# Query, key and gate projections as units of seven half-size products

## The chip, the cores and the metric

The kernel runs on one core of a Trainium2 chip. The metric is the device time of one execution, in microseconds. The core's engines are named as the profile names them: PE is TensorE (matrix products), PEld its weight loads, DVE is VectorE, ACT is ScalarE, POOL is GpSimd, SP is SyncE, which here only issues DMAs.

## The reference

One encoder layer for 512 tokens with 2048 features, in fp32:

```python
h = rms_norm(x, norm_mix_w)
q_a, k_a, v_a, q_g, k_g, v_g, r_g, gate_lr = split_cols(h @ w_in, IN_SPLITS)   # 1024,1024,1024,512,512,1024,1024,16
y_a = chunked_band_attention(q_a, k_a, v_a, att_rel_bias)      # 16 heads of 64, chunks of 64, own chunk + 8 before it
o_g = gated_linear_attention(q_g, k_g, v_g, log_a)             # 4 heads, keys of 128, values of 256
y_g = rms_norm(o_g, gla_norm_w) * silu(r_g)                    # the gates meet the GLA outputs here
x = x + concatenate([y_a, y_g]) @ w_out
u_gate, u_val = split(causal_depthwise_conv(rms_norm(x, norm_ffn_w) @ w_ffn_up))   # 2 x 5632 columns
x = x + (gelu(u_gate) * u_val) @ w_ffn_down
g = sigmoid(rms_norm(x, norm_ple_w) @ w_ple_gate)
x = x + g * (p @ w_ple_proj)                                   # per-layer embedding, 256 features
return rms_norm(x, final_norm_w)
```

With 512 tokens and a band of nine chunks of 64 every earlier token is in the band, so each block of 128 queries (`qt` = 0 to 3) meets 128 x (`qt` + 1) keys.

## The kernel before

**Number form.** Every large fp32 product is made of three: each operand is split into a high part (a copy rounded to the type fp32r, by ACT) and a low part (the rest, a subtraction on DVE), and PE forms high x high, high x low and low x high. The activations lie transposed, features on the partitions: 16 tiles of 128 features by 512 tokens.

**First part (0 to about 600 us): full products.** The normalised input is kept as 16 split tiles, `h1`. `vproj` (L218) forms value projections with tokens on the output's partitions, in two column halves `c` of eight weight tiles `kp` each; the products are L240 to L242. `proj` (L127) forms one block of 128 output columns as 16 feature tiles x 3 products of 512 columns, 48 products (`mm3`, L122 to L125). The order is: the GLA values (`Vg`), the low-rank gate, the four GLA heads with two gate blocks (`gate_block`) between, the attention values (`Va`), and then a loop over `b` = 0 to 8. In it block `b` (two heads of 64) gets its query block (`att_q`), the transposes of the probabilities of `b - 1` (`att_transpose`), its key block (`att_k`), the value products of `b - 1` (`att_out`, L496), and its scores and softmax (`att_probs`, L453 to L475), one head after the other; `b` = 8 carries gate blocks 2 and 3 instead of projections. The Tile scheduler orders this part. Each head's queries and keys stand as two stacked halves of 64 partitions: the query tile holds high over low, and for the key's high and low part the same 64 rows twice, both written by ACT or DVE from the projection.

**Border (about 600 to 668 us): a list of blocks in written order.** From here every PE, DVE and ACT instruction is kept in program order (`InOrder`). `blocks` holds, four times, the two weight halves of a gate block and an embedding block `ple` (24 products, `pp`), which it stores to `ppd`. `block_load`, `block_prep` and `block_product` work three, two and no blocks ahead. The lists `before` and `after` hang the rest on the blocks: the multiplication of the GLA outputs by their gates (`gated`), the storing of operands for the next stage (`mix_pair`), and loads and splits of that stage's operands (`wo.load`, `wo.split`).

**Later stages (about 668 us to the end): units of seven half-size products.** A unit takes two blocks of 128 output columns and all 512 tokens as a 2 x 2 block problem and forms it, after Winograd's variant of Strassen's scheme, from seven products instead of eight, each with 256 tokens and half of the features:

```python
PRODUCTS = {"P1": ("L11", "R11", "A"), "P2": ("L12", "R21", "B"), "P6": ("S2", "N2", "A"), "P5": ("S1", "N1", "C"),
            "P7": ("S3", "T3", "A"), "P3": ("S4", "R22", "C"), "P4": ("L22", "T4", "A")}
```

L are weights, S their sums; R are activations, N and T their differences. A product is 8 feature tiles x 3 = 24 matrix products of 256 columns, accumulated in a PSUM bank `accA`, `accB` or `accC`. The seven activation operands are formed once for a stage by `store_pair`, written to DRAM by SP and loaded back (`Stage.load`, `Stage.split`). The weights go through raw pages of 512 KB: `wanted` is the list of loads in order of use, `free` the free pages, and `issue` starts the next load as soon as a page is free. A sum is a plain load from SP and then an adding DMA from POOL's queue onto the same page (L663), or an addition on DVE, as the unit's `sums` says. `prep_high` and `prep_low` split a product's weights two products ahead of it; `collect` adds a finished product to the unit's quarters. The stages are `wo` (w_out), `up`, `dn0` to `dn2` and `pg` (embedding gate). All units' products make up one list `steps`, and `agenda[i]` holds what else is to be issued at step i; its second key says where in the step: 0 before the splits, 1 between the high and the low split, above 1 after the product.

Of the kernel before, what the change touches and what calls it, by code (L numbers as in the profile page):

```python
# [29 lines left out]
            "P7": ("S3", "T3", "A"), "P3": ("S4", "R22", "C"), "P4": ("L22", "T4", "A")}  # L30
# [9 lines left out]
def encoder_block(ctx: ExitStack, tc: tile.TileContext, A, out):  # L40
# [46 lines left out]

    def page(ring, name, dt=F32, shape=(P, 1024)):
        tags = RINGS[ring]
# [127 lines left out]

    def vproj(src, V, start=False):  # L218
        for c in range(2):
            ps = [psum_mm(f"v{c}_{t}") for t in range(TT)]  # L220
            for kp in range(KD // 2):
                first = start and c == 0
                xs = []
                if first and kp > 0:
                    xs.append(load_input(2 * kp))
                hi, lo = wtile(src[c, kp], f"wv{c}_{kp}", 2 if first and kp < 2 else 1,
                               (lambda: xs.append(load_input(0))) if first and kp == 0 else None)
                if first:
                    xs.append(load_input(2 * kp + 1))
                    sq_acc(xs[0], kp == 0)  # L230
                    sq_acc(xs[1], False)
                    if kp == KD // 2 - 1:
                        first_stats()
                for j in range(2):
                    kt = 2 * kp + j
                    wh = hi[:, j * T:(j + 1) * T]
                    wl = lo[:, j * T:(j + 1) * T]
                    for t in range(TT):
                        sl = slice(t * P, (t + 1) * P)
                        nc.tensor.matmul(ps[t], h1[kt][:, 0, sl], wh, start=kt == 0, stop=False)  # L240
                        nc.tensor.matmul(ps[t], h1[kt][:, 0, sl], wl, start=False, stop=False)  # L241
                        nc.tensor.matmul(ps[t], h1[kt][:, 1, sl], wh, start=False, stop=kt == KD - 1)  # L242
            for t in range(TT):
                nc.scalar.activation(V[:, t, c * T:(c + 1) * T], ps[t], AF.Copy, scale=rtok[:, t:t + 1])
# [5 lines left out]
    onorm = []  # L250
# [9 lines left out]
    with ExitStack() as mix:  # L260
        vp = mix.enter_context(tc.tile_pool(name="v", bufs=1, side="right"))

        with ExitStack() as gctx:
            gp = gctx.enter_context(tc.tile_pool(name="gla", bufs=1, side="right"))
            reset = gp.tile([P, T], F32, name="reset")
            nc.gpsimd.memset(reset, 1.0)
            nc.gpsimd.memset(reset.rearrange("p (c j) -> p c j", j=CHUNK)[:, :, 0:1], 0.0)
            causal = gp.tile([P, P], I32, name="causal")
            nc.gpsimd.memset(causal, 1)
            nc.gpsimd.affine_select(causal, causal, pattern=[[1, P]], compare_op=ALU.is_ge, fill=0, base=0, channel_multiplier=-1)  # L270
            attn_t = []
            for i in range(2):
                t = gp.tile([P, T], F32, name=f"attnT{i}")
                nc.gpsimd.memset(t, 0.0)
                attn_t.append(t)

            V = vp.tile([P, TT, 1024], F32, tag="V", name="Vg")
            vproj(A["w_v_g"], V, True)
            up2 = gp.tile([P, T], F32, name="up2")[0:32]
            nc.sync.dma_start(up2, A["gate_up"])  # L280

            gl = page("wr", "wgate_r")
            nc.sync.dma_start(gl[:, :256], A["w_gate"])
            glh = page("wh", "glh", F32R)
            nc.scalar.activation(glh[:, KD * 32:KD * 32 + 96], attn_t[0][:, 0:96], AF.Copy)
            gl3 = gl[:, :256].rearrange("p (k r) -> p k r", r=16)
            g3 = glh[:, :KD * 32].rearrange("p (k r) -> p k r", r=32)
            nc.scalar.activation(g3[:, :, 0:16], gl3, AF.Copy)
            nc.vector.tensor_tensor(g3[:, :, 16:32], gl3, g3[:, :, 0:16].bitcast(F32), ALU.subtract)
            plr = psum_mm("plr")  # L290
            for kt in range(KD):
                w = glh[:, kt * 32:kt * 32 + P]
                nc.tensor.matmul(plr, w, h1[kt][:, 0, :], start=kt == 0, stop=False)
                nc.tensor.matmul(plr, w, h1[kt][:, 1, :], start=False, stop=kt == KD - 1)
            lr = gp.tile([P, T], F32, name="lr")[0:32]
            nc.vector.tensor_tensor(lr, plr[0:32, :], rb[0:32, :], ALU.mult)

            def gt(name, tag, bufs=1, cols=T):
                return gp.tile([P, cols], F32, tag=tag, name=name, bufs=bufs)

            def gla_proj(hd):
                pz = psum_aux("pz")
                nc.tensor.matmul(pz, up2[:, hd * P:(hd + 1) * P], lr, start=True, stop=True)
                b = bgate[:, hd:hd + 1]
                e = gt("e", "e")
                nc.scalar.activation(e, pz, AF.Abs, bias=b)
                nc.scalar.activation(e, e, AF.Exp, scale=-1.0)
                nc.scalar.activation(e, e, AF.Ln, bias=1.0)
                m = gt("lf", "lf")
                nc.vector.tensor_scalar(m, pz, b, 0.0, ALU.add, ALU.min)  # L310
                nc.vector.tensor_tensor(m, m, e, ALU.subtract)
                cs = gt("cs", "cs")
                nc.vector.tensor_tensor_scan(cs, reset, m, 0.0, ALU.mult, ALU.add)
                cs3 = cs.rearrange("p (c j) -> p c j", j=CHUNK)
                last = cs3[:, :, CHUNK - 1:CHUNK]
                eb = gt("eb", "eb", 2)
                nc.scalar.activation(eb, cs, AF.Exp, scale=1.0 / TAU)
                en = gt("en", "en", 2)
                nc.scalar.activation(en, cs, AF.Exp, scale=-1.0 / TAU)
# [830 lines left out]
    for n in range(3):  # L1150
        block_load(n)
# [198 lines left out]
```

## Time and profile before

| | |
|---|---|
| median of 3 runs | 2340.82 us (2331.72 to 2340.89) |
| profiled execution: time, span | 2332.86 us, 2331.2 us |
| mean granted clock of PE | 0.993 |
| busy: PE, PEld | 2294.6 us (98%), 2155.6 us (92%) |
| busy: DVE, ACT, POOL | 1783.8 us (77%), 1231.0 us (53%), 122.7 us (5%) |
| DMA | 473.99 MB, 203 GB/s over the span |

The busy times are of one execution and of engines that work side by side, so they are not added up; the span is the time from the first to the last recorded instruction. "Granted clock" is the share of full speed that the throttle allowed PE. In the rows of groups, `out<-in` are the program's names for the tiles; then come the shapes, the count, the total of busy time, the mean duration in ns, and the idle time before them with what ended it. `L62` is the line of the helper that records all instructions of the part kept in program order. DMA rows give size and median us from issue to landing. In the chain of waits each row is one instruction with its start (us) and the time that it holds in the chain, followed by engine, tile and line; `x48` joins 48 in a row.

### The profile page before, as it was taken

The numbers are of one execution on the slowest core, as the hardware profiler recorded it, in microseconds if no ns is written. First come the engines' busy times: TensorE is split into PE (matmuls) and PEld (weight loads), VectorE is DVE, ScalarE is ACT, GpSimd is POOL, SyncE is SP. The second block draws the span as 40 slices with busy tenths as digits, with TensorE's granted clock in tenths as the row PEclk, the third lists the DMA queues.
The fourth block names the chain that finished last, engine by engine and source line by source line (L and its number), as shares of the span: only waits on it lengthen the run. The fifth ranks groups of instructions, "written<-read, shape, count | busy, mean of one in ns | idle before, by whom it ended". The sixth has DMA issues, their size and how long they took to land.

```text
span 2331.2 us, 42270 instructions
## 1 busy us (share of the span) xinstructions
PE 2294.6 (98%) x16924; PEld 2155.6 (92%) x16924; DVE 1783.8 (77%) x2459; ACT 1231.0 (53%) x1807; POOL 122.7 (5%) x156
## 2 busy tenths in 40 slices
PE   9999999999999999999999999999999999999996
PEld 8878887777789999999999999999999999999995
DVE  6256326656568898999888888888898787998887
ACT  6344225445455565555555555555564554656655
POOL 0000000000000010100000000000000100000000
PEclk9999999999999999999999999999999999999998
DMA  5222222222687987777777777777866967879994
GB/s 204 84 73 73 100 100 97 92 95 78 228 293 255 283 263 205 213 218 221 213 215 209 217 202 221 208 216 198 260 215 226 313 214 243 295 253 329 282 277 153
DMA packets 172821, 473.99 MB, mean 203 GB/s; under 512 B 18736, under 2 KB 58928, under 8 KB 172624
## 3 DMA queue, kind: packets, MB, share of 16 engines
q1 hardware_dynamic: 148112, 392.64, 47.3%
q0 software_dynamic: 20160, 72.36, 17.4%
q10 hardware_dynamic: 4352, 6.29, 0.8%
q8 instruction: 132, 2.16, 0.4%
q14 instruction: 65, 0.53, 0.1%
HBM read 404.11 MB, written 65.01 MB: 201 GB/s over the span
## 4 chain that ended last, share of the span: by engine, by line
PE 92%; DVE 3%; ACT 2%; DMA 1%; issue 1%; SPq 0%; DVEq 0%; ACTq 0%; POOL 0%; POOLq 0%
PE accA L62 37%; PE accC L62 19%; PE accB L62 9%; PE v L240 2%; PE v L241 2%; PE v L242 2%; PE pr L62 2%; PE pqa L123 1%; PE pqa L124 1%; PE pka L125 1%; PE pqa L125 1%; PE pka L123 1%; PE pka L124 1%; PE pp L62 1%; PE py L496 1%
## 5 line engine op out<-in xcount | busy, mean ns | idle before, releaser
L62 DVE TENSOR_TENSOR wl<-s,wh 128x1024 fp32r<-128x1024 f32 (+1 forms) x317 | 379.3, 1197 | 58.0 <-ACT wh L62 57.6
L62 DVE TENSOR_TENSOR wl<-l,wh 128x1024 fp32r<-128x1024 f32 (+1 forms) x268 | 319.5, 1192 | 48.9 <-ACT wh L62 48.4
L62 ACT ACTIVATE wh<-l 128x1024 fp32r<-128x1024 f32 (+1 forms) x268 | 276.9, 1035 | 146.2 <-PE accC L62 99.0
L62 ACT ACTIVATE wh<-s 128x1024 fp32r<-128x1024 f32 (+1 forms) x317 | 327.4, 1033 | 27.4 <-DVE s L62 11.9
L62 ACT ACTIVATE u<-accA 128x256 f32<-128x256 f32 x254 | 96.2, 379 | 352.8 <-PE accA L62 352.7
L62 DVE TENSOR_TENSOR s<-s,l 128x1024 f32<-128x1024 f32 (+1 forms) x168 | 200.5, 1193 | 0.6 <-DMA s<-in_w_dn 0.6
L62 PE MATMUL accA<-up_T,wh 128*128 128x256 f32 x1408 | 178.8, 279 | 0.0
L62 PEld LDWEIGHTS accA<-up_T,wh 128*128 128x128 f32 x1408 | 170.3, 188 | 0.0
L62 DVE SCALAR_TENSOR_TENSOR cv<-u,cw,cv 128x511 f32<-128x511 f32 (+1 forms) x176 | 131.6, 748 | 3.1
L663 POOL DMA_DIRECT2D s<-in_w_up x88 | 75.1, 853 | 791.8 <-DMA s<-in_w_up 371.1
L119 DVE TENSOR_TENSOR wv_l<-wv_r,wv_h 128x1024 fp32r<-128x1024 f32 (+1 forms) x34 | 39.5, 1161 | 84.3 <-ACT wv_h L118 84.2
L240 PE MATMUL v<-wv_h,h 128*128 128x512 f32 x256 | 100.4, 392 | 0.0
L242 PE MATMUL v<-wv_h,h 128*128 128x512 f32 x256 | 100.0, 391 | 0.0
L241 PE MATMUL v<-wv_l,h 128*128 128x512 f32 x256 | 99.6, 389 | 0.0
L62 PE MATMUL accA<-up_T,wl 128*128 128x256 f32 x704 | 96.6, 279 | 0.0
L62 PE MATMUL accB<-up_R,wh 128*128 128x256 f32 x704 | 91.0, 281 | 2.0 <-DVE up_R L62 1.3
L62 PE MATMUL accA<-dn_T,wh 128*128 128x256 f32 x704 | 90.6, 280 | 1.1 <-ACT wh L62 1.1
L62 PE MATMUL accA<-up_R,wh 128*128 128x256 f32 x704 | 89.8, 280 | 0.0
L62 PE MATMUL accC<-up_N,wh 128*128 128x256 f32 x704 | 89.4, 279 | 0.0
L62 PE MATMUL accC<-up_R,wh 128*128 128x256 f32 x704 | 89.4, 279 | 0.0
L62 PE MATMUL accA<-up_N,wh 128*128 128x256 f32 x704 | 89.4, 279 | 0.0
L62 PEld LDWEIGHTS accB<-up_R,wh 128*128 128x128 f32 x704 | 86.3, 189 | 2.6 <-DVE up_R L62 1.5
(394 smaller groups left out, 5280.2 us busy)
## 6 DMA issues: line engine op xcount, KB each, us to landing
l<-in_w_up SPq DMA_DIRECT2D x132, 512.0 KB, 5.2
s<-in_w_up SPq DMA_DIRECT2D x88, 512.0 KB, 4.7
s<-in_w_up POOLq DMA_DIRECT2D x88, 512.0 KB, 5.6
l<-in_w_dn SPq DMA_DIRECT2D x56, 448.0 KB, 5.1
l<-in_w_out SPq DMA_DIRECT2D x28, 512.0 KB, 4.7
l<-in_w_dn SPq DMA_DIRECT2D x28, 512.0 KB, 5.8
l<-in_w_ple_gate SPq DMA_DIRECT2D x24, 512.0 KB, 6.8
g_R<-cv SPq DMA_DIRECT2D x66, 128.0 KB, 4.5
```

What stands on the lines that cost most here:

```text
L62: ins = f(*args, **kw)
L119: nc.vector.tensor_tensor(lo[:, c], raw[:, c], hi[:, c].bitcast(F32), ALU.subtract)
L123: nc.tensor.matmul(po, whi, act[:, 0, :], start=start, stop=False)
L124: nc.tensor.matmul(po, whi, act[:, 1, :], start=False, stop=False)
L125: nc.tensor.matmul(po, wlo, act[:, 0, :], start=False, stop=stop)
L240: nc.tensor.matmul(ps[t], h1[kt][:, 0, sl], wh, start=kt == 0, stop=False)
L241: nc.tensor.matmul(ps[t], h1[kt][:, 0, sl], wl, start=False, stop=False)
L242: nc.tensor.matmul(ps[t], h1[kt][:, 1, sl], wh, start=False, stop=kt == KD - 1)
L496: nc.tensor.matmul(py[s * 64:(s + 1) * 64, kt * P:T], Va[:, kt, c0:c0 + 64], PT[s][:, kt, kt * P:T], start=kt == 0, stop=kt == TT - 1)
L663: nc.gpsimd.dma_start(t, src("L22" if name == "S1" else "L11"), accum_op=ALU.add)
```

## The change

* The 16 query and key blocks become eight units of seven half-size products: unit `u` takes query block `u` and key block `u` as its two blocks of columns. The eight gate blocks become four units. They form a new first stage `in` (`front`), with units one after the other, six raw pages (r0 to r5) and the banks b0 to b2 for the products, b3 for the attention output and b4 to b7 for the rest. The rings of the other pages are cut for its time (`FRONT_RINGS`).
* Its seven activation operands are formed while the second column half of the GLA values runs: `input_pair(k)` scales x in place by the norm's weight and its reciprocal root `rb`, and `store_pair` writes seven operands for each of eight pairs (56 stores of 128 KB).
* During the attention values (`Va`) operand tiles R11, R21 and N2 are loaded back and split (`operand_step`); N1, T3, R22 and T4 are loaded after the last of those products (`operands_left`) and split in the first steps.
* Values and GLA outputs go through DRAM: `Va` is written there and read back for each block (`load_v`), the GLA outputs are written and read back at their gate units (`load`).
* The attention of block `b` is an agenda of its unit (`attend`): high halves by ACT (`high`), low halves by DVE (`low`), the second copy of the key halves by four DMAs on POOL's queue (`double`), and then three groups of query tiles, `TILES`, each for both heads: scores, softmax, scaling, transposes, copy to SBUF, value products.
* Two embedding blocks (step `PP`) stand ahead of the stage's units, and two behind them. The hand-written block list and the loop over `b` go. The rows of w_out are laid out in another order, so that a pair of operands holds blocks 2m and 2m + 1.

The later stages stay as they are. The core of the diff:

```diff
--- before.py
+++ after.py
-RINGS = {"wr": ("r0", "r1", "r2"), "wh": ("h0", "h1", "h2"), "wl": ("l0", "l1", "l2"), "u": ("u2", "u3", "u0", "u1"),
-         "c": ("c1", "c2", "c0"), "x": ("x0", "x1")}
+RINGS = {"wr": ("r0", "r1", "r2"), "wh": ("h0", "h1", "h2"), "wl": ("l0", "l1", "l2")}
+FRONT_RINGS = {"u": ("u0", "u1"), "c": ("c0",), "x": ("r6",)}
+BACK_RINGS = {"u": ("u2", "u3", "u0", "u1"), "c": ("c1", "c2", "c0"), "x": ("x0", "x1")}
...
-    def gate_block(j):
-        pr = psum_mm("pr")
-        proj(pr, [A["w_blk"][24 + j, i] for i in range(2)], h1, f"wr{j}")
-        r = tp.tile([P, T], F32, tag="sq", name="r")
-        nc.vector.tensor_tensor(r, pr, rb, ALU.mult)
-        nc.scalar.activation(r, r, AF.Silu)
-        nc.vector.tensor_tensor(onorm[j], onorm[j], r, ALU.mult)
...
-            def att_q(b):
-                pq = psum_mm("pqa")
-                proj(pq, [A["w_blk"][b, i] for i in range(2)], h1, f"wqa{b}")
-                qf = ap.tile([P, T], F32, tag="qkf", name="qf")
-                nc.vector.scalar_tensor_tensor(qf, pq, 0.125, rb, ALU.mult, ALU.mult)
-                Q = [ap.tile([P, T], F32R, tag=f"Q{s}", name=f"Q{s}") for s in range(2)]
-                for s in range(2):
-                    a, z = s * 64, 64 - s * 64
-                    nc.scalar.activation(Q[s][a:a + 64], qf[a:a + 64], AF.Copy)
-                    nc.vector.tensor_tensor(Q[s][z:z + 64], qf[a:a + 64], Q[s][a:a + 64].bitcast(F32), ALU.subtract)
...
-            def att_k(b):
-                pk = psum_mm("pka")
-                proj(pk, [A["w_blk"][8 + b, i] for i in range(2)], h1, f"wka{b}")
-                kf = ap.tile([P, T], F32, tag="qkf", name="kf")
-                nc.vector.tensor_tensor(kf, pk, rb, ALU.mult)
-                Kh = [ap.tile([P, T], F32R, tag=f"Kh{s}", name=f"Kh{s}") for s in range(2)]
-                Kl = [ap.tile([P, T], F32R, tag=f"Kl{s}", name=f"Kl{s}") for s in range(2)]
-                for s in range(2):
-                    a, z = s * 64, 64 - s * 64
-                    nc.scalar.activation(Kh[s][a:a + 64], kf[a:a + 64], AF.Copy)
-                    nc.scalar.activation(Kh[s][z:z + 64], kf[a:a + 64], AF.Copy)
-                    nc.vector.tensor_tensor(Kl[s][a:a + 64], kf[a:a + 64], Kh[s][a:a + 64].bitcast(F32), ALU.subtract)
-                    nc.vector.tensor_tensor(Kl[s][z:z + 64], kf[a:a + 64], Kh[s][a:a + 64].bitcast(F32), ALU.subtract)
...
-    free = ["r8"] + [f"r{i}" for i in range(3, 8)]
+    free = [f"r{i}" for i in (3, 4, 5)]
-    banks = [f"b{i}" for i in range(6)]
+    banks = [f"b{i}" for i in range(3)]
...
+    def embedding(unit):
+        hi, lo = unit.w["PP"]
+        for i in range(4):
+            if i % 2 == 0:
+                o = (early[0].tile([P, 1024], F32, tag="pp_o", name="pp_o", bufs=4) if unit.u < 2 else page("c", "pp_o"))
+                o = o.rearrange("p (s t) -> p s t", s=2)
+            pp = psum_aux("pp")
+            for k in range(2):
+                w = slice((i * 2 + k) * P, (i * 2 + k + 1) * P)
+                product3(pp, hi[:, w], lo[:, w], ps_[0][:, k], k == 0, k == 1)
+            act.activation(o[:, i % 2, :], pp, AF.Copy)
+            if i % 2:
+                m = 4 * unit.u + i - 1
+                nc.scalar.dma_start(ppd[m % 8:m % 8 + 2, m // 8].rearrange("m p t -> p m t"), o)
...
+    TILES = ((3,), (2,), (1, 0))
...
+        def high():
+            for n in ("Q", "Kh", "Kl"):
+                for s in range(2):
+                    M[n, s] = tile_(f"{n}{s}", T, F32R)
+            for s in range(2):
+                a = slice(s * 64, s * 64 + 64)
+                act.activation(M["Q", s][a], o[a, 0, :], AF.Copy, scale=0.125)
+                act.activation(M["Kh", s][a], o[a, 1, :], AF.Copy)
+        def low():
+            for s in range(2):
+                a, z = slice(s * 64, s * 64 + 64), slice(64 - s * 64, 128 - s * 64)
+                vec.scalar_tensor_tensor(M["Q", s][z], o[a, 0, :], 0.125, M["Q", s][a].bitcast(F32), ALU.mult, ALU.subtract)
+                vec.tensor_tensor(M["Kl", s][a], o[a, 1, :], M["Kh", s][a].bitcast(F32), ALU.subtract)
+        def double():
+            for s in range(2):
+                a, z = slice(s * 64, s * 64 + 64), slice(64 - s * 64, 128 - s * 64)
+                for n in ("Kh", "Kl"):
+                    nc.gpsimd.dma_start(M[n, s][z], M[n, s][a])
+        def scores(h):
+            for s in range(2):
+                psc = M["psc", s, h] = psum_aux("psc")
+                for i, qt in enumerate(TILES[h]):
+                    w = slice(256 * i, 256 * i + max(P * (qt + 1), 256))
+                    nn = w.stop - w.start
+                    ql = M["Q", s][:, qt * P:(qt + 1) * P]
+                    ten.matmul(psc[:, w], ql, M["Kh", s][:, :nn], start=True, stop=False)
+                    ten.matmul(psc[:, w], ql, M["Kl", s][:, :nn], start=False, stop=True)
...
+        def normal(h):
+            for s in range(2):
+                for qt in TILES[h]:
+                    sc, mx = M["sc", s, qt], M["mx", s, qt]
+                    vec.reciprocal(mx[:, 3:4], mx[:, 2:3])
+                    vec.tensor_scalar(sc, sc, mx[:, 3:4], None, ALU.mult)
+        def turn(h):
+            for s in range(2):
+                ptr = M["ptr", s] = psum_aux("ptr")
+                for i, qt in enumerate(TILES[h]):
+                    for kt in range(qt + 1):
+                        ten.transpose(ptr[:, (2 * i + kt) * P:(2 * i + kt + 1) * P], M["sc", s, qt][:, kt * P:(kt + 1) * P], ident)
...
+        def values(h):
+            if h == 0:
+                M["y"] = pp_.tile([P, T], F32, tag="b3", name="py")
+            for i, qt in enumerate(TILES[h]):
+                for kt in range(qt + 1):
+                    for s in range(2):
+                        o = (2 * i + kt) * P
+                        ten.matmul(M["y"][s * 64:(s + 1) * 64, qt * P:(qt + 1) * P], M["V"][:, kt, s * 64:(s + 1) * 64],
+                                   M["PT"][:, s, o:o + P], start=kt == 0, stop=kt == qt)
...
+        items = [(2, 0, load_e), (2, 2, high), (3, 1, low), (3, 3, double), (4, 1, mask), (5, 0, load_v), (11, 1, result)]
+        if b % 2:
+            items.append((12, 1, lambda: store_pair(mixd, b // 2, ypair[0][:, 0, :], ypair[0][:, 1, :])))
+        for h in range(3):
+            items += [(t + h, k, lambda f=f, h=h: f(h)) for t, k, f in (
+                (5, 6, scores), (6, 1, soft), (7, 1, normal), (7, 5, turn), (8, 1, evict), (8, 4, values))]
+        return items
...
+        return [(0, 0, load), (0, 1, lambda: act.activation(unit.o, unit.o, AF.Silu)), (0, 2, times), (0, 3, pair)]
...
+    front = Stage("in", list(range(12)), 8, h1d, front_weights, lambda u: (attend if u.u < 8 else after_gates)(u), "dma",
+                  "dma", single=True)
+    embed = [Stage("pp", us, 8, None, lambda u, q: A["w_ple_proj"][u], lambda u: [], "dma", "dma", single=True)
+             for us in ([0, 1], [2, 3])]
+    for u in embed[0].units + embed[1].units:
+        u.order, u.uses, u.made = ("PP",), dict(L11=1), set()
...
+    stages[:0] = [embed[0], front, embed[1]]
...
+    for n, op in enumerate(("T3", "R22", "T4")):
+        for g in range(2):
+            agenda[n + g * (n == 2)].append((3, lambda op=op, g=g: front.split(op, g)))
...
+            def input_pair(k):
+                for i in (k, k + 8):
+                    x = xslot(i, "")
+                    vec.scalar_tensor_tensor(x, x, nmix[:, i:i + 1], rb, ALU.mult, ALU.mult)
+                store_pair(h1d, k, xslot(k, ""), xslot(k + 8, ""), gp.tile([P, 1024], F32, tag="tp", name="tp", bufs=2))
+            for c in range(2):
+                vproj(A["w_v_g"], c, lambda t: V[:, t, c * T:(c + 1) * T], c == 0, input_pair if c else None)
...
+    def operand_step(kp):
+        if kp > 1:
+            front.split(*X0[kp - 2])
+        if kp == 3:
+            embedding_split(raws["p"], early[0].tile([P, 2, 1024], F32R, tag="ps", name="ps"))
+            issue()
+    def operands_left():
+        hctx.close()
+        xb.append(ctx.enter_context(tc.tile_pool(name="xb", bufs=1, reuse_waits="tile")))
+        pad = xb[0].tile([P, 8], F32, tag="pad", name="pad")
+        nc.gpsimd.memset(pad, 0.0)
+        for op in ("N1", "T3", "R22", "T4"):
+            for g in range(2):
+                front.load(op, g)
+        free.extend(("r0", "r1", "r2"))
+        issue()
+        prep(0)
+        prep(1)
+        for g in range(2):
+            front.split("N1", g)
+    values_a(1, operand_step, operands_left)
...
```

More of the change, by code (lines that the diff above doesn't have):

```diff
@@ L936, in encoder_block @@
                 u.paired = len(group) > 1
-            need = [[(u, name) for name in NEEDS[u.sums]] for u in group]
+            need = [[(u, name) for name in (NEEDS[u.sums] if u.stage not in embed else ("L11",))] for u in group]
             wanted += [e for es in zip(*need) for e in es]
@@ L941, in encoder_block @@
     now = [0]
[L942 removed]
+    for a, b in zip(stages[3:], stages[4:]):
         i0 = base[a.units[-1]]
```

678 lines of the change are left out of this document (320 added, 358 removed).

## The prediction

> **What bounds the kernel now.** I read the page first (engines, slices, chain), then the chain in order of time, then busy time by stage, then the grouped rows of the stages that the change touches.
>
> ```profile
> span 2331.2 us, 42270 instructions
> PE 2294.6 (98%) x16924; PEld 2155.6 (92%) x16924; DVE 1783.8 (77%) x2459; ACT 1231.0 (53%) x1807; POOL 122.7 (5%) x156
> DMA  5222222222687987777777777777866967879994
> PE 92%; DVE 3%; ACT 2%; DMA 1%; issue 1%; SPq 0%; DVEq 0%; ACTq 0%; POOL 0%; POOLq 0%
> ```
> ```profile
> 387.74 2.31 PE py L496 x16
> ...
> 568.03 2.30 PE py L496 x16
> ...
> 584.33 1.78 PE ptr L485 x16
> ...
> 618.36 10.92 PE pr L62 x48
> 629.28 5.60 PE pp L62 x24
> ...
> 667.99 9.26 DMA wo_N<-mix_N
> ...
> 1361.72 5.60 PE accA L62 x48
> ```
> ```profile
> 51.00:94.00 43.00, 43.00 (x192) 35.57 (x191) 9.00 (x8) 10.13 (x14) 0.00 (x0) 1.00 0.25 85
> 338.00:600.00 262.00, 261.27 (x1281) 203.62 (x1279) 150.22 (x443) 129.05 (x280) 0.00 (x0) 1.00 0.26 87
> 600.00:694.00 94.00, 89.86 (x478) 76.12 (x477) 61.28 (x90) 48.55 (x74) 3.97 (x6) 1.00 0.90 302
> 900.00:1600.00 700.00, 700.00 (x6002) 700.00 (x6001) 613.72 (x733) 373.82 (x506) 59.87 (x71) 1.00 0.76 214
> ```
>
> TensorE (PE) is busy 98% of the span and makes 92% of the chain, so time falls only if PE gets less to do and nothing new makes it wait. The stage table (window, its length, busy PE, PEld, DVE, ACT, POOL, granted clock, DMA share, GB/s) says where there is room. In the attention stage (338 to 600 us) PE is full, VectorE (DVE) has 150 of 262 us, the DMAs move 87 GB/s and GpSimd (POOL) does nothing. The up-projection (900 to 1600 us), already made of half-size products, shows what that form costs the others: DVE 614 of 700 us and 214 GB/s, with PE still full. The clock is 1.00 in all of these windows.
>
> The sum is made against the profiled execution: 2332.9 us, of which the span is 2331.2. That lies 8 us (0.34%) under the median of 2340.8 shown and near the lowest run, 2331.7; if the new kernel is timed at the level of the median, its time is 8 us more. About 0.5% (12 us) is what a measurement of this kernel can tell from no change.
>
> **The products themselves.** Before, a block of 128 columns is 48 full products: 10.92 us in the chain, 227.5 ns each. Twenty-four blocks go (16 query and key, 8 gate): 24 x 10.92 = 262.1 us. In their place come 12 units of 7 x 24 half-size products. A run of 48 of those takes 5.60 us, 116.7 ns each, so a unit is 19.6 us and twelve are 235.2 us. Difference **-26.9 us**, 2.24 per unit. All of it lies on the path.
>
> The Trainium skill ("TensorE: Matmul & The Clock Gate", section "Back-to-back issue gap") gives the isolated gap as N / 2.4 + 2.5 ns: an estimate from that page is 215.8 and 109.2 ns, and the difference would be -28.5 us. The same section says that real streams are paced by the weight load too. The trace differs from the formula (227.5 and 116.7 ns), and the rows decide.
>
> **Scores, transposes, values.** Between the value products of block 0 and of block 6 lie 180.3 us, 30.05 per block. Two projections are 21.84 of that, so the rest of a block's attention takes 8.2 us of PE, switches between product kinds included. The change keeps the same score widths and the same 20 transposes. The values become 20 products of 128 columns where 8 wider ones were, with the same columns in all (1280 a head), and the two heads still alternate. I take no change, -0.3 to +2 us a block. A unit then needs 19.6 + 8.2 = **27.8 us** of PE, eight times.
>
> **DVE beside it.** These are a unit's rows, from the attention stage (eight blocks) and from the up-projection:
>
> ```profile
> L449 DVE TENSOR_TENSOR Kl<-kf,Kh 64x512 fp32r<-64x512 f32 x16 | 11.0, 686 | 0.2
> ...
> L467 DVE CUSTOM_DVE_ANT_0 sc<-psc,E 128x512 f32<-128x512 f32 x16 | 10.9, 681 | 0.0
> L471 DVE RECIPROCAL mx<-mx 128x1 f32<-128x1 f32 x64 | 9.4, 159 | 4.6 <-ACT sc L470 4.6
> L467 DVE CUSTOM_DVE_ANT_0 sc<-psc,E 128x384 f32<-128x384 f32 x16 | 8.8, 553 | 0.3
> L469 DVE TENSOR_SCALAR mx<-mx 128x1 f32<-128x1 f32 x64 | 8.4, 141 | 0.0
> L472 DVE TENSOR_SCALAR sc<-sc,mx 128x512 f32<-128x512 f32 x16 | 7.8, 486 | 0.2
> L467 DVE CUSTOM_DVE_ANT_0 sc<-psc,E 128x256 f32<-128x256 f32 x16 | 6.7, 420 | 0.0
> L472 DVE TENSOR_SCALAR sc<-sc,mx 128x384 f32<-128x384 f32 x16 | 6.7, 419 | 0.0
> L472 DVE TENSOR_SCALAR sc<-sc,mx 128x256 f32<-128x256 f32 x16 | 5.6, 348 | 0.0
> L429 DVE SCALAR_TENSOR_TENSOR qf<-pqa,rb 128x512 f32<-128x512 f32 x8 | 5.5, 692 | 12.5 <-PE pqa L125 12.5
> ...
> L467 DVE DVE_READ_ACCUMULATOR2_ANT mx<- 128x1 f32 x64 | 5.3, 83 | 0.0
> ...
> L467 DVE CUSTOM_DVE_ANT_0 sc<-psc,E 128x128 f32<-128x128 f32 x16 | 4.6, 286 | 0.2
> L472 DVE TENSOR_SCALAR sc<-sc,mx 128x128 f32<-128x128 f32 x16 | 4.5, 282 | 0.0
> ```
> ```profile
> L62 DVE TENSOR_TENSOR wl<-s,wh 128x1024 fp32r<-128x1024 f32 x122 | 148.9, 1220 | 8.9 <-ACT wh L62 8.9
> ...
> L62 DVE TENSOR_TENSOR s<-s,l 128x1024 f32<-128x1024 f32 x62 | 75.6, 1219 | 0.0
> ...
> L62 DVE TENSOR_TENSOR u<-u,accB 128x256 f32<-128x256 f32 x30 | 12.6, 420 | 0.2 <-PE accB L62 0.2
> ```
>
> The softmax rows (L467, L469, L471, L472) add up to 78.7 us for eight blocks, 9.8 a block. The low halves of Q and K take 4 x 0.69 = 2.7. The unit's weights need 7 low parts and 2 sums at 1.22 (11.0), its quarters 3 additions at 0.42 (1.3), and every second block makes operand differences, 4 x 0.42 (0.8 on average). Together 25.6 of 27.8 us, 92%: it fits, though only just, and now in an order written out by hand (before, the scheduler mixed it).
>
> The tight place is the third group of transposes, which PE reaches four products after the first scores. From those scores to there DVE has 3 low parts and 2 sums (6.1), one addition (0.4) and the whole softmax (9.8): 16.3 us. PE has 4 x 2.8 plus the 8.2 without the first scores (4 x 227.5 ns, 0.9), the last six of 20 transposes (0.11 each, 0.7) and the last six of 20 value products (0.3 of 2.31, 0.7), so 11.2 + 5.9 = 17.1 us. The spare of 0.8 goes in the blocks that also form the differences (1.7). I charge 0.5 us a unit, **+4 us**, with bounds 0 and 2 a unit. The four gate units carry no attention of their own (DVE some 15 of 19.6 us): nothing.
>
> **Weights and copies.** A unit reads 7 tiles of 512 KB where four were, and has six pages to hold them; the later stages have nine. A sum page is two DMAs in a row, a plain load and then an adding one from POOL's queue.
>
> ```profile
> l<-in_w_up SPq DMA_DIRECT2D x132, 512.0 KB, 5.2
> s<-in_w_up SPq DMA_DIRECT2D x88, 512.0 KB, 4.7
> s<-in_w_up POOLq DMA_DIRECT2D x88, 512.0 KB, 5.6
> ...
> g_R<-cv SPq DMA_DIRECT2D x66, 128.0 KB, 4.5
> ```
> ```profile
> L663 POOL DMA_DIRECT2D s<-in_w_up x88: 844/857/878, 820.9 to 1661.5; - x88
> ```
> ```profile
> DMA to landing us min/median/max: 7.2/9.1/15.0
> ```
>
> The next unit's S1 gets its page when this unit's S4 is made, and is wanted when S2 is made four steps on. PE takes 14.1 us for those (four products 11.2, first scores 0.9, last transposes 0.7, two groups of values 1.3), and DVE uses 1.7 of them until S4 is there: 12.4 us. By the up-projection's rows the chain takes 4.7 + 5.6 = 10.3, so 2 are spare; by the last row (the adding loads from 600 to 840 us, beside 302 GB/s) it is 4.7 + 9.1 = 13.8, or 1.4 late. A unit moves about 5.4 MB (3.7 weights, 0.5 bias, 0.3 values, 0.5 copies, 0.5 stores) in 27.8 us, 195 GB/s, nearest to the up-projection's 214: I charge nothing, bounds 0 and 1.4 a unit.
>
> The doubled halves of K, made by ACT and DVE before, become four copies on POOL's queue. Each occupies POOL 0.86 us by the row above, and two stand behind S1's adding load. They have from the end of the low halves to the first scores, two products and a half or 7 us; behind a 5.6 us landing plus two issues that is 7.3. No row shows such a copy. I take 0 because DVE is mostly earlier than that; it could cost up to 3 a unit, and where something else makes PE wait there first it costs nothing.
>
> **Borders.** While the second half of the GLA values is made (51 to 94 us), DVE also forms the operands: 8 x (2 x 0.69 + 4 x 0.42) = 24.5 us beside the 9.0 shown, of 43, and SP issues 56 stores of 128 KB, with the weight tiles 5 to 7 queued behind the stores of pairs 4 to 6. At 4.5 us to landing and two buffers of differences, tile 5 just arrives: **+1**, 0 to 6. At the entry, eight operand tiles (4.2 MB, 14 us at the 302 GB/s shown) can land only after the last value product. Two embedding blocks cover 11.2 us and three products on tiles already there 8.4 more, but DVE splits T3 ahead of P2's low part: **+2**, 0 to 6. At the exit PE before sat idle 4.1 us (94.0 less 89.9 busy, 600 to 694 us), behind operand loads that land late (9.26 in the chain). After the change two embedding blocks still stand there, and the loads crowd the same way: 0, -4 to +5. The four embedding blocks (5.60 each) stay on PE in all; two are only moved ahead of the units, and their stores, 2 MB on ACT's queue, now go out among the operand loads (within the 2 above).
>
> **Sum.** -26.9 + 4 + 1 + 2 = -20, so 2332.9 - 20 = **2313 us**; its own range is 2302 (no new wait, the old exit wait gone) to 2325.
>
> **Rivals.** *1, slower: S1 comes late.* DVE runs in program order, so a late S1 holds the softmax, which holds the transposes, and each microsecond goes to PE. With the longest adding load of the row (15.0) the chain is 19.7, 7.3 late in eight units: 2313 + 58 = 2371. It decides from 12.4 us on; the result is slower by 0.5% from about 16.4. For it: six pages, and POOL's queue shared with the copies. Against: 195 GB/s, and the up-projection had the same pair of DMAs with PE full. Chance 0.16.
>
> *2, DVE becomes the bound.* Written order and waits on itself stretch the 25.6 us to the 30.05 that a block took before. The attention units then gain nothing, the gates 4 x 2.24 = 9.0: 2332.9 - 9.0 + 3 = 2327, no change by the bound. For it: 92% before any wait. Against: 88% in the up-projection cost PE nothing. Chance 0.14.
>
> *3, POOL is locked out.* DVE's scaling of the probabilities holds POOL off; the last four scalings, 2 x (0.35 + 0.28) = 1.3 us, stand just ahead of the K copies, which then land that much later in each of eight units: 2313 + 10 = 2323, no change by the bound. No row shows POOL issuing beside L472. Chance 0.06. The Trainium skill ("SBUF — State Buffer", section "Who interferes with whom") states such a lock: tensor_scalar in a two-port mode and GpSimd's descriptor writing exclude each other, which speaks against moving these copies to that queue. No run here shows it yet.
>
> The forecast keeps 0.64. The changed code forms every query, key and gate block in a unit, so that it does not do what it says is no case here. Faster by over 0.5%: 0.66 (a little of rival 3 added); within: 0.18; slower: 0.16. The range to hold 8 in 10 takes in rivals 2 and 3 and leaves out 1: 2302 to 2340.
>
> **What would show it.** Right: `accA`, `accB`, `accC` fed by `in_` tiles at 5.60 us per 48, value products 27.8 to 28.5 us apart, DVE about 90% busy there, POOL no longer idle. Rival 1: `s2` waiting for a POOL DMA; rival 2: `ptr` or `py` waiting for DVE with DVE full; rival 3: POOL issues well over 0.86 us. A wait of `psc` for the copies over 1 us a unit, or over 6 us of PE idle at the entry, would break the sum.

## The result, and the profile after

The changed kernel takes 2327.71 us (median of 20 runs, 2320.9 to 2340.74) where the kernel before takes 2335.72 us (20 runs, 2329.77 to 2346.49): ratio 0.9966, 95% interval 0.9951 to 0.9981. It is faster by 8 us, 0.34%. The forecast was 20 us. The profiled execution took 2329.97 us.

The page of the changed kernel, with the rows that answer to those of before:

```profile
span 2328.3 us, 44943 instructions
PE 2273.8 (98%) x17980; PEld 2190.4 (94%) x17980; DVE 1879.8 (81%) x2557; ACT 1287.6 (55%) x1878; POOL 161.1 (7%) x212
DMA  6622577777897987788777777777866967879894
PE 82%; DVE 7%; DMA 6%; ACT 3%; issue 2%; SPq 0%; POOL 0%; ACTq 0%; DVEq 0%; POOLq 0%
```
```profile
51.00:94.00 43.00, 43.00 (x192) 35.55 (x191) 30.42 (x56) 10.13 (x14) 0.00 (x0) 1.00 0.77 248
338.00:600.00 262.00, 253.26 (x2164) 241.59 (x2166) 209.55 (x494) 164.51 (x326) 34.12 (x51) 0.97 0.71 191
600.00:694.00 94.00, 87.85 (x691) 83.84 (x688) 73.88 (x96) 58.55 (x87) 5.99 (x7) 1.00 0.96 309
900.00:1600.00 700.00, 700.00 (x6002) 700.00 (x6001) 613.28 (x732) 375.82 (x511) 61.43 (x72) 1.00 0.78 213
```

PE is busy for 20.8 us less than before (2294.6), but the chain of waits is no longer nearly all PE: DMAs hold 6% of it, DVE 7%. The stage table says where. From 338 to 600 us PE is busy 253.3 of 262 us (261.3 before), and the granted clock in that window is 0.97, where it was 1.00. The up-projection is as it was. While the GLA values run (51 to 94 us) DVE went from 9.0 to 30.4 us with PE still full: forming the operands there costs nothing.

What PE waited for between 330 and 600 us (engine, tile, what released it: total, times, longest):

```profile
PE psc L64 <- DMA Kl<-Kl: 5.8, 3, 3.4
PE accA L64 <- ACT u L64: 4.1, 1, 4.1
PE psc L64 <- DVE s L64: 0.9, 1, 0.9
PE ptr L64 <- DVE mx L64: 0.4, 2, 0.2
PE py L64 <- ACT PT L64: 0.4, 1, 0.4
```

Two waits make up most of it. The chain in order of time shows both (start, length, what), first at the entry, then at the first scores of units 0 and 1:

```profile
325.13 9.27 DMA ppd<-pp_o
...
334.47 0.37 ACTq L687
...
338.78 0.28 ACT u L64
...
339.10 5.49 PE accA L64 x24
...
370.06 0.60 POOL s L404
370.67 6.08 DMA Kl<-Kl
...
376.78 0.80 PE psc L64
377.58 4.97 PE accA L64 x24
...
398.56 0.52 POOL Kl L731
399.08 8.07 DMA Kl<-Kl
```

*The entry.* ACT issues the stores of the embedding blocks (`ppd`) and runs in written order. The fourth store was issued at 334.47, just after the second had landed (325.13 + 9.27). Behind it ACT had the splits of R22 and T4, and the emptying of bank `accA` (`u`, 338.78), which PE needed for N2. The next product could have started at 334.8 and started at 339.1, 4.3 us late.

*The first scores.* The copy of K's low half was issued right behind S1's adding load (`s`, L404) on POOL's queue and landed 6 to 8 us later. In unit 0 PE sat idle 3.4 us for it, and the next product started 3.9 us late. There the copy was also issued late: DVE had written the half at 367.1, but POOL, which issues in order too, stood at the adding load until S1's plain load had landed (369.5), and issued the copy at 370.7.

Behind both, a product of 24 holds the chain for 5.49 and 4.97 us where it takes 2.80; from start to start it is 5.3 and 5.0. The stage table of these stretches (last three columns: granted clock, DMA share, GB/s):

```profile
331.00:334.50 3.50, 3.50 (x32) 3.50 (x32) 0.27 (x1) 0.00 (x0) 0.00 (x0) 1.00 1.05 390
334.50:339.00 4.50, 0.47 (x4) 0.26 (x3) 3.03 (x3) 4.12 (x6) 0.00 (x0) 0.87 1.07 396
339.00:344.00 5.00, 4.90 (x23) 4.90 (x24) 5.00 (x6) 2.89 (x4) 0.00 (x0) 0.50 0.37 127
373.00:376.70 3.70, 0.39 (x2) 0.00 (x0) 0.89 (x2) 0.00 (x0) 0.32 (x1) 0.82 1.08 223
376.70:382.00 5.30, 5.22 (x23) 5.12 (x24) 4.27 (x12) 1.61 (x4) 0.00 (x0) 0.50 0.52 141
```

After each stall PE ran some 5 us at a granted clock of 0.50. So each costs its length and 2.2 to 2.5 us more in this execution: 4.3 + 2.5 at the entry, 3.9 + 2.2 in unit 0. (In another execution of the same kernel, `e11_changed_again`, a wait of 4.3 us in unit 0 was followed by 3.4 us at 0.50 and cost 1.5 more.)

### The profile page after: what moved, and what is told of

Read it like the earlier page. It is cut to its first block, busy times and chain, and to the rows that moved or that the text cites. A ratio compares the mean times of both kernels' runs of the same rounds, so it can differ in the third digit from the quotient of the medians.

```text
span 2328.3 us, 44943 instructions
## 1 busy us (share of the span) xinstructions
PE 2273.8 (98%) x17980; PEld 2190.4 (94%) x17980; DVE 1879.8 (81%) x2557; ACT 1287.6 (55%) x1878; POOL 161.1 (7%) x212
## 3 DMA queue, kind: packets, MB, share of 16 engines
q0 software_dynamic: 26176, 89.14, 21.4%
## 4 chain that ended last, share of the span: by engine, by line
PE 82%; DVE 7%; DMA 6%; ACT 3%; issue 2%; SPq 0%; POOL 0%; ACTq 0%; DVEq 0%; POOLq 0%
PE accA L64 38%; PE accC L64 19%; PE accB L64 10%; PE v L249 3%; PE v L251 2%; PE v L250 2%; DVE wl L64 2%; DMA Kl<-Kl 1%; DMA s<-in_w_blk 1%; DVE s L64 1%; DMA s<-in_w_dn 1%; DVE u L64 1%; PE pk L133 1%; PE pk L132 1%; PE pk L134 1%
## 5 line engine op out<-in xcount | busy, mean ns | idle before, releaser
L64 DVE TENSOR_TENSOR wl<-s,wh 128x1024 fp32r<-128x1024 f32 (+1 forms) x365 | 437.8, 1200 | 67.4 <-ACT wh L64 66.5
L64 DVE TENSOR_TENSOR wl<-l,wh 128x1024 fp32r<-128x1024 f32 (+1 forms) x308 | 368.5, 1196 | 73.3 <-ACT wh L64 72.6
L64 ACT ACTIVATE wh<-l 128x1024 fp32r<-128x1024 f32 (+1 forms) x308 | 319.2, 1037 | 182.5 <-PE accC L64 120.0
L64 ACT ACTIVATE wh<-s 128x1024 fp32r<-128x1024 f32 (+1 forms) x365 | 378.0, 1037 | 36.0 <-DVE s L64 16.6
L64 ACT ACTIVATE u<-accA 128x256 f32<-128x256 f32 x290 | 110.0, 379 | 378.0 <-PE accA L64 377.5
L64 DVE TENSOR_TENSOR s<-s,l 128x1024 f32<-128x1024 f32 (+1 forms) x192 | 229.7, 1196 | 8.7 <-DMA s<-in_w_blk 8.7
L404 POOL DMA_DIRECT2D s<-in_w_up x88 | 75.1, 853 | 790.3 <-DMA s<-in_w_up 363.3
L64 ACT ACTIVATE u<-accC 128x256 f32<-128x256 f32 x94 | 36.0, 383 | 106.6 <-PE accC L64 106.5
L64 PEld LDWEIGHTS accA<-dn_T,wh 128*128 128x128 f32 x704 | 86.5, 190 | 4.8 <-ACT wh L64 4.8
```

What stands on the lines that cost most here:

```text
L64: ins = f(*args, **kw)
L404: nc.gpsimd.dma_start(t, src("L22" if name == "S1" else "L11"), accum_op=ALU.add)
```

## The experiments

Each kernel is compared with the kernel before on the same chip; where three were run beside each other, their medians are compared too.

### Each stall by itself

The changed kernel as it is:

> The changed kernel as it is, as the yardstick for the three edits beside it. 2320 to 2335 us; a stall of some 4 us in front of the fourth product of the first unit and late key copies in several units, of varying length.

Measured 2324.76 us, ratio 0.9952 (0.9934 to 0.9969), with the same two stalls; the longest waits for `u` and `Kl` were 4.3 and 3.4 us (4.1 and 3.4 above).

**The stores.** Only the queue of the first four embedding stores changes:

```diff
-nc.scalar.dma_start(ppd[...], o)
+(nc.gpsimd if unit.u < 2 else nc.scalar).dma_start(ppd[...], o)
```

> The four stores of the first two embedding blocks go to POOL's queue instead of ACT's; nothing else moves. Theory A: ACT, in written order, was held 3.9 us at the fourth of these stores, which could be issued only when the second had landed (9.3 us), and the splits of R22 and the emptying of accA stood behind it; then the stall of 4.3 us ahead of the first N2 product and the later one of 2.2 us in that unit go, and the time falls by 4 to 6.5 us. Theory B: the operand tiles themselves land late at 370 to 400 GB/s; then the wait of ACT only changes its name and the time stays within 1.5 us.

Measured 2318.96 us, 5.8 below the yardstick, ratio 0.9933 (0.9915 to 0.9951). The stores land no sooner; what PE waits for between 330 and 600 us is now

```profile
PE psc L64 <- DMA Kl<-Kl: 6.4, 3, 4.6
PE py L64 <- ACT PT L64: 0.4, 1, 0.4
PE ptr L64 <- DVE mx L64: 0.2, 1, 0.2
```
```profile
L687 POOL DMA_DIRECT2D ppd<-pp_o x4: 710/734/757, 321.8 to 330.2; - x4
...
DMA to landing us min/median/max: 6.8/8.2/9.4
```

The wait for `u` is gone although the DMAs are as slow as before (8.2 us to landing, where the first four took 7.9; 389 GB/s from 322 to 338 us): the operand tiles had landed, and it was ACT that was held. Theory A. Why the fourth store waited for the second, though the four have buffers of their own, is told by the trace's records of these instructions. On ACT's queue the second and the fourth store report their landing on the same semaphore, and ACT waits for that semaphore ahead of the fourth; on POOL's queue each of the four has a semaphore of its own. So ACT was held by a wait that came with the reuse of a semaphore. What the edit gave up: the longest wait for the copies grew from 3.4 to 4.6 us.

**The copies.** From SP's queue instead of POOL's, with the instructions of PE, DVE and ACT unchanged:

```diff
-nc.gpsimd.dma_start(M[n, s][z], M[n, s][a])
+nc.sync.dma_start(M[n, s][z].bitcast(F32), M[n, s][a].bitcast(F32))
```

> The four copies that double the halves of K are issued from SP's queue instead of POOL's; PE, DVE and ACT run the same instructions in the same order. Theory A: the copies of the low halves came late (7 to 10 us from issue to landing) because they stood behind S1's adding load of 512 KB in POOL's queue; then they land in about 4 to 5.5 us, the first scores stop waiting for them in all eight units (8.6 us in the profiled run), and the time falls by 5 to 9 us. Theory B: they are late from the traffic of 190 to 230 GB/s as such; then they take 7 us or more on SP's queue too and the time stays within 2 us.

Measured 2321.45 us, 3.3 below the yardstick, ratio 0.9944 (0.9924 to 0.9965). The landing times of the low halves, first of the changed kernel, then of this one:

```profile
DMA to landing us min/median/max: 5.7/7.2/9.7
```
```profile
DMA to landing us min/median/max: 3.0/4.4/6.1
```

So the copies were late from the queue in which they stood, not from the traffic, and no unit's first scores wait any more. The median gains less than expected, but its six runs lie between 2317 and 2328 us; in the trace the stage for `w_out` starts at 651.6 us where the yardstick's starts at 659.4, and these 7.8 us are as expected. In unit 0 the third wait in line came forward, `ptr` waiting 1.0 us for a softmax that stood behind a late S1.

**The halves by engines**, as in the kernel before:

```diff
 act.activation(M["Kh", s][a], o[a, 1, :], AF.Copy)
+act.activation(M["Kh", s][z], o[a, 1, :], AF.Copy)
...
 vec.tensor_tensor(M["Kl", s][a], o[a, 1, :], M["Kh", s][a].bitcast(F32), ALU.subtract)
+vec.tensor_tensor(M["Kl", s][z], o[a, 1, :], M["Kh", s][a].bitcast(F32), ALU.subtract)
...
-(3, 3, double),
```

> No copies by DMA: the second halves of K are written by ACT (2 x 0.6 us) and DVE (2 x 0.7 us) as in the kernel before. Theory A (the copies are what the units wait for, and DVE has room at 80% busy): the waits of the first scores go, the time falls by 4 to 9 us as with SP's queue. Theory C (DVE bounds the units, rival 2): each unit gets 1.4 us longer, the time rises by 3 to 11 us.

Measured 2318.27 us, 6.5 below the yardstick, ratio 0.9926 (0.9909 to 0.9943). Between 360 and 600 us PE's waits come down to

```profile
PE ptr L64 <- DVE mx L64: 0.4, 2, 0.2
PE py L64 <- ACT PT L64: 0.4, 1, 0.4
```

and the units follow each other at 27.57 us, seven times. The 1.4 us of DVE's time a unit cost nothing. The interval of each edit alone overlaps the yardstick's; what carries the verdicts is that each named wait is gone from its trace, and the sum, next.

### Both together

> Both edits together: the first embedding stores on POOL's queue, the second halves of K by ACT and DVE. If the two stalls are separate and add up (each with the stretch at half clock behind it), it is 5.8 + 6.5 = 12 us below the changed kernel: 2311 to 2314 us, ratio to before near 0.990; no wait of PE over 1.5 us is left between 330 and 635 us and the eight units follow each other at 27.6 us. If one stall only hid the other (the S1 page or the operand tiles are the next thing late), the gain stops at 6 to 8 us.

Measured 2317.18 us, ratio 0.9899 (0.9877 to 0.992): the ratio as expected, the time 3 us above. No wait of PE over 1.2 us is left between 330 and 635 us, and the units follow each other at 27.57 us.

> The first embedding stores on POOL's queue and the key copies on SP's queue. Queue theory: as good as with the engines' halves, 2311 to 2315 us, with the copies landing in 4 to 5 us and DVE 1.4 us a unit less busy. If copies and SP's loads get in each other's way, 2 to 5 us slower than with the engines' halves.

Measured 2320.67 us, ratio 0.9917 (0.9898 to 0.9936): 3.5 us slower than with the engines' halves by the median, and `w_out` starts 6.6 us later (650.6 against 644.0), as expected if copies and loads get in each other's way. S1 is late in the first units (DVE waited 13.3 us for `s` between 330 and 430 us, 5.4 with the engines' halves).

Again, with the changed kernel beside it:

> Both edits again, beside the changed kernel on the same chip: 10 to 13 us below it if the two stalls add up, ratio to before 0.989 to 0.992.

> The changed kernel again, the yardstick for the three beside it: ratio to before 0.995 to 0.997; the stalls of 4.3 us at the entry and of 3 to 5 us at the first scores, each with some 5 us at a granted clock of 0.50 behind it, are there again.

Measured 2310.19 us (ratio 0.9893, 0.9871 to 0.9916) and 2329.75 us (0.9966, 0.9952 to 0.9979). Two edits of a line or two bring 17 to 20 us by these figures, and this version beats both kernels, by 25 us against the kernel before (1.07%). Some of the 20 is not the edits': in the profiled execution of the changed kernel the up-projection alone took 8.1 us longer than in the other (the last section shows the two paces). When the stage for `w_out` starts (first product `accA<-wo_R`; columns: ns, first and last start) shows it, in the kernel before, the changed one, and both edits:

```profile
L62 PE MATMUL accA<-wo_R,wh x128: 277/280/384, 668.6 to 794.3; 128*128 128x256 f32 x128
```
```profile
L64 PE MATMUL accA<-wo_R,wh x128: 277/279/280, 662.8 to 789.8; 128*128 128x256 f32 x128
```
```profile
L64 PE MATMUL accA<-wo_R,wh x128: 277/279/280, 643.4 to 770.1; 128*128 128x256 f32 x128
```

5.8 us are gained up to there by the change, 25.2 with the two edits. In two more profiled executions of the changed kernel the stage started at 659.4 and 659.6 us, so there the change gains 9, and the two edits gain 16 on top. The single edits gain 5.5 and 8.1 up to there: the stalls add up, and a little more, since the longer wait for the copies that the first edit brought goes with the second.

### Is it the clock?

Sixteen idle products ahead of the first scores of unit 0, in the changed kernel:

```diff
+if b == 0 and h == 0:
+    pf = psum_aux("fill")
+    for _ in range(16): ten.matmul(pf[:, :P], ones, ones, start=True, stop=True)
```

> The changed kernel, with 16 idle products of 128 columns (some 3.4 us on PE) written ahead of the first scores of unit 0, where PE waits 3.8 us for the key copies. If the 5.0 us of the following T product (2.8 elsewhere) come from the clock, granted at 0.50 after the idle stretch, the product is back at 2.8 us with the filler, and the scores end no later: 1 to 2.3 us faster, the entry's stall untouched. If the T product is slow from its operands or weights, it stays at 5 us and the time is the same or up to 3 us longer.

Measured 2325.27 us, ratio 0.9944 (0.9922 to 0.9967), which as a time settles nothing. The trace does: the fill is the first row, the scores with what is left of the wait the second, the product fed by `in_T` the third.

```profile
373.00:376.50 3.50, 3.50 (x34) 3.50 (x33) 0.42 (x1) 0.41 (x1) 0.85 (x1) 1.00 1.04 205
376.50:378.70 2.20, 1.34 (x7) 0.85 (x7) 0.74 (x1) 0.00 (x0) 0.00 (x0) 1.00 0.80 158
378.70:381.50 2.80, 2.80 (x25) 2.78 (x24) 2.73 (x8) 1.48 (x4) 0.00 (x0) 1.00 0.48 116
```

The clock stays at 1.00 and the product takes 2.8 us instead of 5.0, with the same operands: the extra 2.2 us come from the idle stretch. The fall at the entry was not filled in this way.

### How near is DVE to being the bound?

Added subtractions between the second scaling and the third softmax, on top of both edits. First four that read the unit's page:

> Both edits of the kernel with the engines' halves, and in every unit four more DVE subtractions of 0.69 us (low key halves written again with the same values) between the second scaling and the third softmax, so just ahead of the third transposes. By the prediction's sum of durations (27.5 us a unit already, and 2.75 more) DVE is then the bound at 30.2 us a unit: 20 us slower than without them. By the recorded overlap of neighbouring DVE instructions (24.7 us a unit, scalings done 2.4 us before their transposes) the added 2.75 us use up the spare and cost 0.3 us a unit: 1 to 5 us slower.

Measured 2343.89 us, ratio 1.002 (1.0005 to 1.0034): 27 us slower than both edits alone, more than either side expected. The load brought waits of its own: ACT waited 21.4 us (five times, up to 4.3) to write a page that the added instructions still read, and PE stood still some 2 us a unit for ACT. So with the key tiles alone, four and two:

```diff
+for s in range(4 if h == 2 else 0):      # 2 in the other kernel
+    kh, a = M["Kh", s % 2], slice(s % 2 * 64, s % 2 * 64 + 64)
+    vec.tensor_tensor(M["Kl", s % 2][a], kh[a].bitcast(F32), kh[a].bitcast(F32), ALU.subtract)
```

> The load of the last DVE experiment once more, but reading the key tiles alone. There the four added subtractions read the unit's output page, which the unit after next writes from ACT at that time, and ACT waited up to 4.3 us for them: 27 us slower, not all of it DVE's own time. Now four subtractions of 0.69 us between the second scaling and the third softmax, on tiles that nothing reads after. If the sum of durations is the bound (27.5 of 27.6 us a unit used), each unit gets 2.75 us longer: 20 to 24 us slower than with both edits alone. If the recorded overlap is real room (24.7 us used, third scalings 2.4 us ahead), 0.3 us a unit: 1 to 5 us slower.

> The same with two subtractions, 1.37 us a unit, on both edits. If the sum of durations is the bound: 10 to 12 us slower than with both edits alone. If the overlap is room: within 1.5 us of it, since the third scalings stand 2.4 us ahead of their transposes.

Measured 2326.63 us (ratio 0.9954, 0.9938 to 0.997) and 2315.12 us (0.991, 0.9891 to 0.9929), against 2310.19 with neither. The stage table of the units, with none, two and four (behind the window and its length stand PE, PEld and DVE):

```profile
398.00:566.00 168.00, 168.00 (x1488) 161.49 (x1487) 150.53 (x376) 118.15 (x244) 10.19 (x12) 1.00 0.66 180
```
```profile
398.00:566.00 168.00, 168.00 (x1487) 161.50 (x1486) 158.33 (x388) 119.03 (x246) 10.18 (x12) 1.00 0.67 183
```
```profile
398.00:566.00 168.00, 166.60 (x1439) 156.53 (x1438) 160.71 (x386) 115.14 (x239) 10.18 (x12) 1.00 0.63 175
```

With two, DVE is busy 94% and the units in the middle still follow at 27.57 us. Of the 4.9 us of the median the trace shows 2.6 up to the start of `w_out` (646.0 against 643.4), in the first unit with attention (29.0 us against 28.0) and the last (29.7 against 28.2); that is more than the 1.5 expected, and the rest stays open. With four the units take 28.4 to 29.1 us. Those of 28.4 have no gap of DVE over 0.3 us; in every second unit one of 1.1 to 1.2 us is left, where DVE waits for PE. The truth lies between the two theories: there is room for 1.4 us a unit, not for 2.75. As an estimate, 28.4 less 2.75 puts DVE's own need at 25.7 us with the halves of K, and 1.4 less, 24.3, without.

## Why the prediction was wrong, point by point

The direction was right, the size was not: 8 us instead of 20. What failed are two terms of the sum, the copies (put at 0) and the entry (put at 2), and a cost that has no term. That 2328 us lies within 2302 to 2340 is luck: the upper part of that range was there for DVE as the bound and for the lock, and the runs show neither at work.

* **The products, -26.9.** Right. 2.80 us a product, 19.6 a unit; with both edits the start of `w_out` moves by 25.2 us.
* **Scores, values, DVE: 27.8 a unit and +4.** Charged too high. The unit is 27.57 us, and with both edits PE waits 0.4 us in all for a softmax. The sum of 25.6 us for DVE was near the 26.1 that its durations add up to with the copies on SP's queue, and above its need (24.3 by the estimate); that the tight place would cost 0.5 us a unit was not so, and rival 2 decides only from somewhere between 1.4 and 2.75 us more than the engines' halves already add.
* **The copies of K, 0. The first step that failed.** The prediction worked out 7.3 us for copies behind an adding load, against 7 available, and then took 0 "because DVE is mostly earlier". DVE being early was not enough: the copies stand behind S1's adding load on POOL's queue, which is issued when the plain load has landed. They landed in 5.7 to 9.7 us. In unit 1 DVE was indeed early (half written at 398.0, wanted at 407.1: 9.1 us instead of 7), but the copy was issued 1.1 us after that and took 8.1. By the lengths of the units the first scores cost some 8.6 us in eight units, 3.9 of it in unit 0 (6.7 are idle time of PE in the waits shown), and the clock took 2.2 more: some 11 us. The prediction's own sign, `psc` waiting over 1 us, came twice (3.4 and 1.7 us).
* **The entry, +2. The second.** It measured 6.8. The stores on ACT's queue were counted as traffic; what they did was to hold ACT, an engine in written order, for 3.9 us ahead of the emptying of a bank, at the wait for a semaphore that two of them share.
* **The price of a stall. The third, missing altogether.** Every wait was charged at its length. Two of them left PE idle for 3.4 and 4.1 us, and each cost 2.2 to 2.5 us more at half clock. The Trainium skill ("TensorE: Matmul & The Clock Gate", section "Part 1: The HAM clock gate") says that PE's clock falls to half after an idle window of about 3.4 us and comes back after a busy one. The trace agrees only in part: here the clock fell 2.0 and 2.9 us into these two waits, and shorter ones did it too. In the first kernel with four subtractions five of eight waits of 1.9 to 2.4 us were followed by 3.4 us at 0.50; two of the eight, each with the stretch behind it:

```profile
413.75:415.60 1.85, 0.01 (x1) 0.01 (x1) 1.71 (x13) 1.85 (x4) 0.00 (x0) 1.00 0.08 8
416.30:419.50 3.20, 3.20 (x22) 2.87 (x19) 3.09 (x10) 2.93 (x11) 0.00 (x0) 0.50 0.81 250
445.30:447.40 2.10, 0.01 (x1) 0.01 (x1) 1.93 (x14) 1.87 (x4) 0.00 (x0) 1.00 0.11 9
447.50:451.00 3.50, 3.45 (x34) 3.03 (x35) 3.39 (x9) 3.50 (x12) 0.00 (x0) 1.00 0.79 242
```

In the changed kernel a wait of 1.7 us at 520 us was followed by products of 2.80. So a length from which the clock falls isn't shown. The price could be read before the change: the kernel before has a wait of 2.2 us at 2143 us, and behind it:

```profile
2146.10:2152.70 6.60, 5.81 (x27) 5.51 (x27) 6.60 (x11) 4.60 (x9) 0.00 (x0) 0.50 1.04 336
```

* **The GLA values, +1.** 0; PE was full. **The exit, 0.** 1.4 us more in the embedding blocks there.
* **S1 (rival 1).** Its pair of DMAs took 5.1 and 6.9 us by their medians from 340 to 600 us, 12.0 of the 12.4 worked out; DVE waited for it in unit 0 alone (2.8 us) of the eight. Not the cause, though the next thing in line, as the copies on SP's queue showed. **The lock (rival 3).** POOL's issues of adding loads took 0.90 us there, 0.86 before. But none of POOL's issues between 338 and 600 us ran at the same time as a scaling, so the exclusion that the prediction quoted was not put to the test.

Together, up to the start of `w_out` in the profiled execution: -26.9, -1.8 in clean units, +10.8 for the copies, +6.8 at the entry, +0.9 in the first 7 us (which varies by as much between runs), +4.2 in the last attention unit and the first gate unit, +1.4 at the exit, less 1.2 that the kernel before lost there: -5.8, as measured there (-9 in the two other executions). The rest of the 8 us lies within what executions differ by.

## What to carry to other kernels

For each DMA that is moved, ask what stands ahead of it on its queue and, on an engine in written order, what stands behind its issue; being ready early buys little behind either. Charge a stall of PE at its length and look at the granted clock of the stretch behind it: here it cost up to 2.5 us more after waits of 3.4 to 4.3 us, and stretches at half clock came after some waits of 2 us as well. An engine at 94% busy by its records can be full: add a known load on tiles that nobody else needs and see whether the period moves.

## What the runs showed of the hardware

A 128 KB copy inside SBUF lands in 4.4 us (median) from SP's queue and 7.2 from POOL's behind an adding load. A stretch at a granted clock of 0.50 lasted 3.4 or 6.8 us between 300 and 600 us, and began while PE was still waiting or up to 1.4 us after. The records of neighbouring DVE instructions overlap by up to 0.09 us: in the kernel with both edits the durations of a unit add up to 27.5 us of 27.6, while busy time is 24.7.

PE's pace differs by 1% between executions at a granted clock of 1.00. The up-projection of the changed kernel in two executions on the same chip (`e0_changed`, then `e11_changed_again`):

```profile
850.00:1650.00 800.00, 799.73 (x6847) 798.88 (x6846) 693.88 (x834) 428.75 (x582) 69.99 (x83) 1.00 0.77 212
```
```profile
850.00:1650.00 800.00, 800.00 (x6792) 799.52 (x6791) 692.66 (x830) 425.49 (x580) 69.08 (x81) 1.00 0.77 210
```

A unit takes 19.60 us in the first and 19.79 in the second, 8.3 us over the stage. Both paces came on this chip, with other kernels too; what sets them isn't shown. That is as much as the whole effect of the change, and the reason why ratios to the kernel before on the same chip are given here, with the start of `w_out` beside them.
